# Strided attention on one core: VectorE's stream as a loop, two groups placed at once, ten single stores

## The chip, the cores and the metric

The kernel runs on one core of one Trainium2 chip. Its time is what the device takes for one launch, in microseconds (us). The core has five engines with instruction streams of their own: TensorE (PE; its weight loads are shown as PEld), VectorE (DVE), ScalarE (ACT), GpSimd (POOL) and SyncE (SP), which here issues all transfers. Sixteen DMA engines move the data between HBM and the on-chip memory (SBUF); matmul results lie in PSUM.

## The reference, cut to what matters

Every query attends to 16 keys alone, the rows 0, 64, 128, ... of its head:

```python
batch, heads, seq, dim = 8, 12, 1024, 64          # float32, stride 64
attend_positions = np.arange(0, seq, stride)      # 16 positions
...
scores  = np.einsum('bhqd,bhkd->bhqk', q, k) / np.sqrt(dim)
weights = np.exp(scores - np.max(scores, axis=-1, keepdims=True))
weights = weights / (np.sum(weights, axis=-1, keepdims=True) + 1e-10)
result[:, :, i, :] = np.einsum('bhqk,bhkd->bhqd', weights, v)[:, :, 0, :]
```

All of Q is read (25.2 MB), all of the result is written (25.2 MB), and only 0.8 MB of K and V is needed.

## The kernel before, in words

The 96 heads are worked on in 24 groups of four. A group's queries are 1 MB. They are loaded into one of 16 buffers (`big`), and the result of the group is later written over them and stored from there. So the loads of groups 0 to 15 can be issued at once, and the loads of groups 16 to 23 wait until the store that frees their buffer has landed.

One group g goes through the engines like this:

- ACT (`cast_a`) and POOL (`cast_p`) each cast half of the queries to bfloat16 (`qb`).
- VectorE transposes them (`turn_over`, `qt`, L353).
- TensorE forms the scores with the keys (`score_products`, L507). POOL copies the keys of the group from `k_all` to a small tile beforehand (`place_k`, L357).
- VectorE transposes the scores out of PSUM (`spread`, L373) and takes the maximum (L378). POOL subtracts it (L383), ACT takes the exponential (L389), VectorE adds up (L394) and takes the reciprocal (L399), POOL multiplies (`normalise`, L403), and VectorE transposes the weights back (`weights_back`, `w_t`, L409).
- TensorE forms the output products in two halves (L521) with the values that POOL has placed (`place_v`, L363). ACT copies each half from PSUM into the group's buffer (`evict`, L421), and SP stores it (L34).

The order of the work is written out by hand. A loop over steps n runs in the program that builds the kernel; step n does for VectorE: `spread(n)`, `turn_over(n+1)`, `maximum(n)`, `add_up(n-1)`, `weights_back(n-2)`, `invert(n-1)`. The other engines have their own lists in the same step. Each engine executes its list in order; waits between engines are worked out by `plan()`: an operation waits on a semaphore that counts the finished operations of another engine, or on a named one ("gate") that counts one kind of operation alone (`turned`, `wt`, `ev`, `stK`, `stV`).

TensorE's stream is the only one that loops on the chip: after two small products for the values and the scores of groups 0 to 2 comes a loop over groups 0 to 19, two per pass (`round_`, L529 and following). A round does the scores of group g+3 and then the two output halves of group g. Each pass ends with five subtractions from the gates (L552) and the loop's counter and branch (L548). Groups 20 to 23 follow as straight code, the last three without scores.

The stores are issued in the order of the list `order` (L444): groups 0 and 1 one by one, all others two at a time, with the loads of groups 16 to 23 in between. The store of groups 20 and 21 waits for an ACT operation that isn't a gate's; the first such one behind the evictions of group 21 is the first eviction of group 23. The store of groups 22 and 23 is issued last, and the program ends when it has landed.

`addr_align` (L145) places the start of the streams of ACT, VectorE and POOL at a multiple of 128 instructions.

Of the kernel before, what the change touches and what calls it, by code (L numbers as in the profile page):

```python
# [42 lines left out]
class Program:  # L43
# [13 lines left out]
    def op(self, engine, fn, reads=(), writes=(), after=(), lane=None, gate=None, gates=(), looped=False, last=False):  # L57
# [12 lines left out]
        for k in writes:  # L70
# [3 lines left out]
            gate=gate, gates=gates, last=last, looped=looped or engine == "PE",  # L74
# [3 lines left out]
    def plan(self):  # L78
# [43 lines left out]
        for i, o in enumerate(self.ops):  # L122
            transfer = o["lane"] != o["engine"]
            o["step"] = 16 if transfer else int(i in signals or o["engine"] == "PE" or o["last"])
# [7 lines left out]
        return counts, list(carriers)  # L132

    def emit(self, loops):
        nc = self.nc
        engines = {
# [6 lines left out]
        with self.tc.tile_critical(no_gpsimd_drain=True):  # L143
            for e in ("ACT", "DVE", "POOL"):
                engines[e].addr_align(128, max_nops=0)  # L145
            for o in self.ops:
                if o["looped"]:
                    continue
                for gate, n in o["gates"]:
                    engines[o["engine"]].wait_ge(gates[gate], n)  # L150
                for d in o["waits"]:
                    p = self.ops[d]
                    engines[o["engine"]].wait_ge(sems[p["lane"]], p["count"])
                r = o["fn"]()
                if o["gate"]:
                    r.then_inc(gates[o["gate"]], 1)
                elif o["step"]:
                    r.then_inc(sems[o["lane"]], o["step"])
# [8 lines left out]
def kernel(  # L167
# [14 lines left out]
    P = 128  # L182
# [6 lines left out]
    TURN = 2  # L189
    AHEAD = 3  # L190
    LOOPED = 20
# [20 lines left out]
    k_cur = [sb.tile([P, 2, 2, 32], BF16, name=f"k_cur{i}") for i in range(2)]  # L212
    v_cur = [sb.tile([P, 4, D], BF16, name=f"v_cur{i}") for i in range(2)]
# [25 lines left out]
    def store(g, n):  # L239
        b = g % NB  # L240
        op("SP", lambda: send(g, n), lane="out8" if n < 2 and b % 2 else f"out{b // 2}",
           reads=[f"b{i % NB}{h}" for i in range(g, g + n) for h in "ab"])
# [109 lines left out]
    def turn_over(g):  # L352
        op("DVE", lambda: nc.vector.transpose(qt[g % 2].bitcast(I32), qb[g % 4].bitcast(I32)),  # L353
           reads=[f"qb{g % 4}0", f"qb{g % 4}1"], writes=[f"qt{g % 2}"], gate="turned")

    def place_k(g):
        op("POOL", lambda: nc.gpsimd.tensor_copy(  # L357
            out=k_cur[g % 2].rearrange("p f b x -> p (f b x)").bitcast(I32),
            in_=k_all[:, g].rearrange("p f b x -> p (f b x)").bitcast(I32),
        ), reads=["k_zero"] + [f"k{g % 2}{s}" for s in range(4)], writes=[f"k_cur{g % 2}"], gate="stK")  # L360

    def place_v(g):
        op("POOL", lambda: nc.gpsimd.tensor_copy(  # L363
            out=v_cur[g % 2].rearrange("p x d -> p (x d)").bitcast(I32),
            in_=v_all[:, g].rearrange("p x d -> p (x d)").bitcast(I32),
        ), reads=[f"v_all{g % 2}{x}" for x in range(4)], writes=[f"v_cur{g % 2}"], gate="stV")

    def scores(g):
        op("PE", None, reads=[f"qt{g % 2}", f"k_cur{g % 2}"], writes=[f"sc{g % 2}"],
           gates=[("turned", g + 1), ("stK", g + 1)])  # L370

    def spread(g):
        op("DVE", lambda: nc.vector.transpose(  # L373
            s_t[g % 2].rearrange("p n k -> p (n k)"), sc_ps[g % 2],
        ), reads=[f"sc{g % 2}"], writes=[f"s_t{g % 2}"])

    def maximum(g):
        op("DVE", lambda: nc.vector.tensor_reduce(  # L378
            out=top[g % 2], in_=s_t[g % 2], op=ALU.max, axis=mybir.AxisListType.X,
        ), reads=[f"s_t{g % 2}"], writes=[f"top{g % 2}"])  # L380
# [7 lines left out]
    def raise_(g):  # L388
        op("ACT", lambda: nc.scalar.activation(  # L389
            out=ex[g % 2][:, :, 0:NK], in_=diff[g % 2], func=AF.Exp, bias=0.0, scale=scale,  # L390
        ), reads=[f"diff{g % 2}"], writes=[f"ex{g % 2}"])

    def add_up(g):
        op("DVE", lambda: nc.vector.tensor_reduce(  # L394
            out=total[g % 2], in_=ex[g % 2], op=ALU.add, axis=mybir.AxisListType.X,
        ), reads=[f"ex{g % 2}"], writes=[f"total{g % 2}"])

    def invert(g):
        op("DVE", lambda: nc.vector.reciprocal(rec[g % 2], total[g % 2]),  # L399
           reads=[f"total{g % 2}"], writes=[f"rec{g % 2}"])  # L400

    def normalise(g):
# [3 lines left out]
        ), reads=[f"ex{g % 2}", f"rec{g % 2}"], writes=[f"w_n{g % 2}"])  # L406

    def weights_back(g):
        op("DVE", lambda: nc.vector.transpose(  # L409
            _ap_with(w_t[g % 2], [w_t[g % 2].ap[0], [64, 8], [1, 2], [2, 32]]),  # L410
            w_n[g % 2].rearrange("p n k -> p (n k)"),
        ), reads=[f"w_n{g % 2}"], writes=[f"w_t{g % 2}"], gate="wt")

    def outputs(g, h):
        op("PE", None, reads=[f"w_t{g % 2}", f"v_cur{g % 2}"], writes=[f"o{h}"],
           gates=[("ev", 2 * g + h + 1)] + ([("wt", g + 1), ("stV", g + 2)] if h == 0 else []))
# [15 lines left out]
    for s in range(4):  # L432
# [11 lines left out]
    order = [("S", 0, 1), ("S", 1, 1), ("S", 2, 2), ("L", 16, 1), ("L", 17, 1), ("S", 4, 2), ("L", 18, 1), ("L", 19, 1),  # L444
             ("S", 6, 2), ("L", 20, 1), ("L", 21, 1), ("S", 8, 2), ("L", 22, 1), ("L", 23, 1)]
# [14 lines left out]
    def on(f, g, *a):  # L460
        if 0 <= g < NG:
            f(g, *a)

    for n in range(NG + 4):
        on(evict, n - 3, 1)
        if n < NG:
            spread(n)
        if n == 0:
            maximum(n)
        on(turn_over, n + 1)  # L470
        if n == 0:
            value_blocks(0, range(2, 4))
        elif n < NG:
            maximum(n)
        on(add_up, n - 1)
        on(weights_back, n - 2)
        on(invert, n - 1)
# [6 lines left out]
        on(scores, n + 1)  # L484
# [14 lines left out]
    def pe_stream(sems, gates):  # L499
        pe = nc.tensor  # L500

        def score_products(g):
            for f in range(2):
                for e in range(2):
                    for b in range(2):
                        c = 2 * b + e
                        r = pe.matmul(  # L507
                            sc_ps[g % 2][32 * c : 32 * c + 32], lhsT=k_cur[g % 2][:, f, b],
# [6 lines left out]
            r.then_inc(sems["PE"], 1)  # L515

        def output_products(g, h):
            for t in range(4):
                for b in range(2):
# [4 lines left out]
                        rhs=v_cur[g % 2][half_b].rearrange("p x d -> p (x d)"),  # L524
# [3 lines left out]

        def round_(g, less, more):  # L529
            if more:  # L530
                pe.wait_ge(gates["turned"], g + AHEAD + 1 - less)
                pe.wait_ge(gates["stK"], g + AHEAD + 1 - less)
                score_products(g + AHEAD)
            for h in range(2):
                pe.wait_ge(gates["ev"], 2 * (g - less) + h + 1)
                if h == 0:
                    pe.wait_ge(gates["wt"], g - less + 1)
                    pe.wait_ge(gates["stV"], g - less + 2)
                output_products(g, h)
# [4 lines left out]
        for g in range(AHEAD):  # L544
            pe.wait_ge(gates["turned"], g + 1)
            pe.wait_ge(gates["stK"], g + 1)
            score_products(g)
        with pe.Fori(0, LOOPED // TURN):  # L548
            for j in range(TURN):
                round_(j, 0, True)  # L550
# [46 lines left out]
```

## Time and profile before

| | us |
|---|---|
| median of 3 runs | 127.99 (127.95 to 128.06) |
| the profiled execution | 128.59 |
| its span, first to last instruction | 126.8 |
| busy: DVE / ACT / POOL / PE | 100.0 / 90.1 / 86.7 / 64.8 |
| moved by DMA | 51.18 MB, mean 404 GB/s over the span |

A page of the profile has these parts: the busy time of each engine, the span in 40 slices, the DMA queues, the chain of work that ended last (followed back from the last instruction), groups of instructions by line, and DMA issues by line. "DVE qt L353" is an operation of VectorE that writes the tile `qt`, issued by line 353. A table by stretches gives for each stretch the busy time of PE, PEld, DVE, ACT and POOL in us with the number of instructions, then TensorE's granted clock, the share of the 16 DMA engines that was busy, and GB/s. A row "x2: 558/592/627, 31.1 to 34.8" of one line's instructions means two of them, with minimum, median and maximum duration in ns, and the start of the first and the last in us; "DMA to landing" is the time from such an issue to its last byte's arrival. An engine's name with a q (DVEq, PEldq, SPq) means a step that its sequencer does alone.

### The profile page before, as it was taken

The numbers are of one execution on the slowest core, as the hardware profiler recorded it, in microseconds if no ns is written. First come the engines' busy times: TensorE is split into PE (matmuls) and PEld (weight loads), VectorE is DVE, ScalarE is ACT, GpSimd is POOL, SyncE is SP. The second block draws the span as 40 slices with busy tenths as digits, with TensorE's granted clock in tenths as the row PEclk, the third lists the DMA queues.
The fourth block names the chain that finished last, engine by engine and source line by source line (L and its number), as shares of the span: only waits on it lengthen the run. The fifth ranks groups of instructions, "written<-read, shape, count | busy, mean of one in ns | idle before, by whom it ended". The sixth has DMA issues, their size and how long they took to land.

```text
span 126.8 us, 1795 instructions
## 1 busy us (share of the span) xinstructions
PE 64.8 (51%) x580; PEld 33.7 (27%) x580; DVE 100.0 (79%) x159; ACT 90.1 (71%) x106; POOL 86.7 (68%) x132
## 2 busy tenths in 40 slices
PE   0000713277788777779535478877774537910000
PEld 0000100043344543334222234454331225500000
DVE  4329699999999999999999999999999997200000
ACT  4025778579988889988999988888997877840000
POOL 4016742899999999999999999999999685200000
PEclk9999999999999999999999655555559995596555
DMA  2999999999999999999998999999899999999991
GB/s 59 341 406 432 455 413 444 434 413 465 393 444 444 403 385 447 413 460 408 413 450 357 424 481 401 393 470 424 382 429 426 424 429 429 413 434 424 424 398 57
DMA packets 6230, 51.18 MB, mean 404 GB/s; under 512 B 3696, under 2 KB 3696, under 8 KB 3696
## 3 DMA queue, kind: packets, MB, share of 16 engines
q1 hardware_dynamic: 6224, 51.12, 96.7%
q14 instruction: 5, 0.04, 0.2%
q8 instruction: 1, 0.02, 0.0%
HBM read 25.95 MB, written 25.17 MB: 403 GB/s over the span
## 4 chain that ended last, share of the span: by engine, by line
DVE 70%; DMA 6%; ACT 5%; PE 3%; SPq 2%; issue 1%; POOL 1%
DVE qt L353 20%; DVE w_t L409 12%; DVE total L394 11%; DVE s_t L373 11%; DVE top L378 11%; DMA big<-in_V_dram 6%; DVE rec L399 4%; ACT big L421 3%; PE o L521 3%; DVE v_all L331 2%; SPq L34 1%; ACT qb L344 1%; PE o L307 1%; POOL big L315 1%; ACT big L323 1%
## 5 line engine op out<-in xcount | busy, mean ns | idle before, releaser
L521 PE MATMUL o<-v_cur,w_t 64*64 64x256 bf16 x384 | 40.9, 379 | 22.0 <-ACT big L421 13.3
L421 ACT COPY big<-o 128x1024 f32<-128x1024 f32 x48 | 46.3, 1015 | 7.4 <-PE o L521 7.1
L521 PEld LDWEIGHTS o<-v_cur,w_t 64*64 64x64 bf16 x384 | 30.0, 148 | 41.6 <-ACT big L421 30.0
L403 POOL TENSOR_TENSOR w_n<-ex,rec 128x512 bf16<-128x512 f32 x24 | 25.4, 1057 | 7.5 <-DVE rec L399 7.5
L507 PE MATMUL sc<-qt,k_cur 128*32 128x512 bf16 x192 | 23.2, 576 | 11.9 <-DVE qt L353 11.8
L383 POOL TENSOR_TENSOR diff<-s_t,top 128x512 f32<-128x512 f32 x24 | 25.4, 1060 | 5.6 <-DVE top L378 5.6
L353 DVE STREAM_TRANSPOSE qt<-qb 128x1024 int32<-128x1024 int32 x24 | 29.1, 1212 | 0.0
L349 POOL CAST qb<-big 128x1024 bf16<-128x1024 f32 x24 | 25.3, 1053 | 0.1
L344 ACT CAST qb<-big 128x1024 bf16<-128x1024 f32 x24 | 25.2, 1054 | 0.0
L409 DVE STREAM_TRANSPOSE w_t<-w_n 128x512 bf16<-128x512 bf16 x24 | 18.2, 759 | 1.3 <-POOL w_n L403 1.2
L389 ACT ACTIVATE ex<-diff 128x512 f32<-128x512 f32 x24 | 15.3, 639 | 5.2 <-POOL diff L383 5.2
L394 DVE TENSOR_REDUCE total<-ex 128x32 f32<-128x544 f32 x24 | 17.2, 718 | 0.3 <-ACT ex L389 0.3
L373 DVE STREAM_TRANSPOSE s_t<-sc 128x512 f32<-128x512 f32 x24 | 16.1, 670 | 0.0
L378 DVE TENSOR_REDUCE top<-s_t 128x32 f32<-128x512 f32 x24 | 15.8, 659 | 0.1
L507 PEld LDWEIGHTS sc<-qt,k_cur 128*32 128x32 bf16 x192 | 3.2, 104 | 22.6 <-DVE qt L353 22.6
L307 PE MATMUL o<-big,perm_v 128*128 128x384 bf16 x4 | 1.5, 521 | 12.7 <-POOL big L315 12.7
L399 DVE RECIPROCAL rec<-total 128x32 f32<-128x32 f32 x24 | 7.7, 320 | 0.0
L357 POOL COPY k_cur<-k_all 128x64 int32<-128x64 int32 x24 | 5.7, 237 | 2.1 <-ACT k_all L300 1.8
L363 POOL COPY v_cur<-v_all 128x128 int32<-128x128 int32 x24 | 7.1, 294 | 0.0
L290 ACT CAST big<-big 128x384 bf16<-128x384 f32 x1 | 0.5, 512 | 5.4 <-DMA big<-in_K_dram 5.4
L291 POOL CAST big<-big 128x384 bf16<-128x384 f32 x1 | 0.5, 509 | 5.1 <-DMA big<-in_K_dram 5.1
L307 PEld LDWEIGHTS o<-big,perm_v 128*128 128x128 bf16 x4 | 0.4, 131 | 13.1 <-POOL big L315 12.7
(18 smaller groups left out, 18.9 us busy)
## 6 DMA issues: line engine op xcount, KB each, us to landing
big<-in_Q_dram SPq DMA_DIRECT2D x24, 1024.0 KB, 14.0
out_dram<-big SPq DMA_DIRECT2D x11, 2048.0 KB, 16.3
out_dram<-big SPq DMA_DIRECT2D x2, 1024.0 KB, 16.6
big<-in_K_dram SPq DMA_DIRECT2D x1, 384.0 KB, 6.6
big<-in_V_dram SPq DMA_DIRECT2D x1, 384.0 KB, 8.0
```

Of the source, the lines that this page charges most:

```text
L344: op("ACT", lambda: nc.scalar.copy(b[:, half:], q[:, half:]), reads=[f"b{g % NB}{h}" for h in "ab"], writes=[f"qb{g % 4}1"])
L349: op("POOL", lambda: nc.gpsimd.tensor_copy(out=b[:, 0:half], in_=q[:, 0:half]), reads=[f"b{g % NB}{h}" for h in "ab"], writes=[f"qb{g % 4}0"])
L353: op("DVE", lambda: nc.vector.transpose(qt[g % 2].bitcast(I32), qb[g % 4].bitcast(I32)), reads=[f"qb{g % 4}0", f"qb{g % 4}1"], writes=[f"q ...
L373: op("DVE", lambda: nc.vector.transpose(s_t[g % 2].rearrange("p n k -> p (n k)"), sc_ps[g % 2],), reads=[f"sc{g % 2}"], writes=[f"s_t{g % ...
L378: op("DVE", lambda: nc.vector.tensor_reduce(out=top[g % 2], in_=s_t[g % 2], op=ALU.max, axis=mybir.AxisListType.X,), reads=[f"s_t{g % 2}"] ...
L383: op("POOL", lambda: nc.gpsimd.tensor_tensor(out=diff[g % 2], in0=s_t[g % 2], in1=top[g % 2].unsqueeze(2).to_broadcast([P, 32, NK]), op=AL ...
L394: op("DVE", lambda: nc.vector.tensor_reduce(out=total[g % 2], in_=ex[g % 2], op=ALU.add, axis=mybir.AxisListType.X,), reads=[f"ex{g % 2}"] ...
L403: op("POOL", lambda: nc.gpsimd.tensor_tensor(out=w_n[g % 2], in0=ex[g % 2][:, :, 0:NK], in1=rec[g % 2].unsqueeze(2).to_broadcast([P, 32, N ...
L409: op("DVE", lambda: nc.vector.transpose(_ap_with(w_t[g % 2], [w_t[g % 2].ap[0], [64, 8], [1, 2], [2, 32]]), w_n[g % 2].rearrange("p n k -> ...
L421: op("ACT", lambda: nc.scalar.copy(to, o), reads=[f"o{h}"], writes=[f"b{g % NB}{'ab'[h]}"], gate=None if g == NG - 1 else "ev")
L507: r = pe.matmul(sc_ps[g % 2][32 * c : 32 * c + 32], lhsT=k_cur[g % 2][:, f, b], rhs=_ap_with(qt[g % 2], [qt[g % 2].ap[0], [D, 8], [16 * D, ...
L521: r = pe.matmul(o_ps[h][half_b, t // 2, 256 * (t % 2) : 256 * (t % 2) + 256], lhsT=w_t[g % 2][half_b, 4 * h + t], rhs=v_cur[g % 2][half_b] ...
```

## The change

- VectorE's steps 2 to 21 are a loop on the chip: five passes of four rounds (`dve_stream`). The steps 0 and 1 stand ahead of it and the steps from 22 on behind it, as straight code. The loop waits on gates alone: new ones count score products (`sc`), POOL's casts (`qp`), exponentials (`ex`), normalised weights (`wn`) and VectorE's own transposes and sums (`own`). Each pass ends with five subtractions from them.
- So that `qp` stands for both halves of a cast, POOL's cast of group g waits for ACT's as well (from group 3 on).
- POOL places keys and values for two groups at once, every second group (from group 2 on), into four tiles instead of two; in its step `place_k` comes first and `place_v` ahead of `normalise`. TensorE no longer waits on `stK` and `stV` in its rounds.
- TensorE's loop covers all 24 groups, four per pass, with three subtractions. The rounds of groups 21 to 23 therefore do score products too, for groups that do not exist; they read the tiles as they are, and nothing reads what they write. VectorE releases them with three `nop`s behind its reciprocal of group 22.
- Groups 0 to 9 are stored one by one; each buffer's store has a semaphore of its own.
- POOL's stream starts 112 instructions behind a multiple of 128.

```diff
-            for e in ("ACT", "DVE", "POOL"):
-                engines[e].addr_align(128, max_nops=0)
+            for e, at in (("ACT", 0), ("DVE", 0), ("POOL", 112)):
+                engines[e].addr_align(128, offset=at, max_nops=0)
...
-    TURN = 2
+    TURN = 4
+    FIRST, LAST, ROUNDS = 2, 22, 4
     AHEAD = 3
-    LOOPED = 20
...
-           reads=[f"b{g % NB}{h}" for h in "ab"], writes=[f"qb{g % 4}0"])
+           reads=[f"b{g % NB}{h}" for h in "ab"] + [f"qb{g % 4}1"] * (g > FIRST), writes=[f"qb{g % 4}0"], gate="qp")
...
+    def place(to, from_, g, n, needs, writes):
+        dims = " ".join("pgabx"[: len(to.shape)])
+        flat = f"{dims} -> p ({dims[2:]})"
+        op("POOL", lambda: nc.gpsimd.tensor_copy(
+            out=to[:, g % 4 % 2 : g % 4 % 2 + n].rearrange(flat).bitcast(I32),
+            in_=from_[:, g : g + n].rearrange(flat).bitcast(I32),
+        ), reads=needs, writes=writes)
+
+    def pair(g):
+        return 1 if g < 2 else 0 if g % 2 else 2
...
-    order = [("S", 0, 1), ("S", 1, 1), ("S", 2, 2), ("L", 16, 1), ("L", 17, 1), ("S", 4, 2), ("L", 18, 1), ("L", 19, 1),
-             ("S", 6, 2), ("L", 20, 1), ("L", 21, 1), ("S", 8, 2), ("L", 22, 1), ("L", 23, 1)]
+    order = [("S", 0, 1), ("S", 1, 1)]
+    for g in range(2, 10, 2):
+        order += [("S", g, 1), ("S", g + 1, 1), ("L", NB + g - 2, 1), ("L", NB + g - 1, 1)]
     order += [("S", g, 2) for g in range(10, 22, 2)]
...
+        if n == NG - 1:
+            for g in range(AHEAD):
+                op("DVE", lambda: nc.vector.nop(), gate="turned", late=True)
+        on(place_k, n + 2)
         on(cast_p, n + 2)
         if n < NG:
             subtract(n)
+        on(place_v, n - 1)
         on(normalise, n - 1)
-        on(place_k, n + 2)
-        on(place_v, n - 1)
...
-        with pe.Fori(0, LOOPED // TURN):
+        with pe.Fori(0, NG // TURN):
             for j in range(TURN):
-                round_(j, 0, True)
-            for name, n in (("turned", 1), ("stK", 1), ("stV", 1), ("wt", 1), ("ev", 2)):
+                pe.wait_ge(gates["turned"], j + AHEAD + 1)
+                score_products(j + AHEAD)
+                for h in range(2):
+                    pe.wait_ge(gates["ev"], 2 * j + h + 1)
+                    if h == 0:
+                        pe.wait_ge(gates["wt"], j + 1)
+                    output_products(j, h)
+            for name, n in (("turned", 1), ("wt", 1), ("ev", 2)):
                 pe.sem_inc(gates[name], -n * TURN)
-        for g in range(LOOPED, NG):
-            round_(g, LOOPED, g + AHEAD < NG)
...
+    def dve_stream(sems, gates):
+        dve = nc.vector
+        with dve.Fori(0, (LAST - FIRST) // ROUNDS):
+            for j in range(ROUNDS):
+                g = FIRST + j
+                dve.wait_ge(gates["sc"], g + 1)
+                lay(g).then_inc(gates["own"], 1)
+                dve.wait_ge(gates["qp"], g + 2)
+                turn(g + 1).then_inc(gates["turned"], 1)
+                dve.wait_ge(gates["own"], 2 * j + 1)
+                highest(g).then_inc(sems["DVE"], 1)
+                dve.wait_ge(gates["ex"], g)
+                sums(g - 1).then_inc(gates["own"], 1)
+                dve.wait_ge(gates["wn"], g - 1)
+                back(g - 2).then_inc(gates["wt"], 1)
+                dve.wait_ge(gates["own"], 2 * j + 2)
+                inverse(g - 1).then_inc(sems["DVE"], 1)
+            for name in ("sc", "qp", "ex", "wn"):
+                dve.sem_inc(gates[name], -ROUNDS)
+            dve.sem_inc(gates["own"], -2 * ROUNDS)
+        prog.rest(sems, gates, {name: LAST - FIRST for name in ("sc", "qp", "ex", "wn")})
```

`lay`, `turn`, `highest`, `sums`, `back` and `inverse` issue the same instructions as `spread`, `turn_over`, `maximum`, `add_up`, `weights_back` and `invert` before.

More of the change, by code (lines that the diff above doesn't have):

```diff
@@ L143, in emit @@
         with self.tc.tile_critical(no_gpsimd_drain=True):
-            for e in ("ACT", "DVE", "POOL"):
-                engines[e].addr_align(128, max_nops=0)
+            for e, at in (("ACT", 0), ("DVE", 0), ("POOL", 112)):
+                engines[e].addr_align(128, offset=at, max_nops=0)
             for o in self.ops:
[L147 to L158, printed above, removed]
+                if not o["looped"] and not o["late"]:
+                    self.put(o, sems, gates, {})
             nc.sync.wait_ge(sems["ACT"], counts["ACT"])
@@ L362, in place_v @@
-    def place_v(g):
[L363 to L366, printed above, removed]
-    def scores(g):
[L369 to L375, printed above, removed]
@@ new lines, in place_v, with lay @@
+    def place_v(g):
+        n = pair(g)
+        if n:
+            place(v_two[g % 4 // 2], v_all, g, n,
+                  [f"v_all{i % 2}{x}" for i in range(g, g + n) for x in range(4)],
+                  [f"v_cur{i % 4}" for i in range(g, g + n)])
+    def scores(g):
+        op("PE", None, reads=[f"qt{g % 2}", f"k_cur{g % 4}"], writes=[f"sc{g % 2}"],
+           gates=[("turned", g + 1)], gate="sc")
+    def lay(g):
+        return nc.vector.transpose(s_t[g % 2].rearrange("p n k -> p (n k)"), sc_ps[g % 2])
```

135 lines of the change are left out of this document (78 added, 57 removed).

## The prediction

> **What bounds the kernel now.** I read the page from the top: span, DMA queues, the chain that ended last. Then the stretches at the end, where engines have stopped.
>
> ```profile
> span 126.8 us, 1795 instructions
> q1 hardware_dynamic: 6224, 51.12, 96.7%
> DVE 70%; DMA 6%; ACT 5%; PE 3%; SPq 2%; issue 1%; POOL 1%
> ```
>
> The chain says VectorE (DVE), 70% of the span. The queue line says that data packets alone fill 96.7% of 16 engines' span. Both cannot set the end, so I look at what runs last.
>
> ```profile
> 104.00:108.00 4.00, 2.65 (x24) 1.95 (x24) 2.88 (x6) 3.32 (x4) 2.73 (x4) 0.59 1.01 422
> 112.00:116.00 4.00, 0.00 (x0) 0.00 (x0) 0.00 (x0) 0.46 (x1) 0.00 (x0) 0.87 1.02 434
> 123.00:123.50 0.50, 0.00 (x0) 0.00 (x0) 0.00 (x0) 0.00 (x0) 0.00 (x0) 0.50 0.77 328
> 123.50:124.00 0.50, 0.00 (x0) 0.00 (x0) 0.00 (x0) 0.00 (x0) 0.00 (x0) 0.50 0.47 197
> 124.00:124.50 0.50, 0.00 (x0) 0.00 (x0) 0.00 (x0) 0.00 (x0) 0.00 (x0) 0.50 0.23 98
> 124.50:125.00 0.50, 0.00 (x0) 0.00 (x0) 0.00 (x0) 0.00 (x0) 0.00 (x0) 0.50 0.23 98
> ```
>
> The columns are PE, PEld, DVE, ACT and POOL busy, granted clock, DMA share, GB/s. From 112.5 us nothing computes; the ring of stores drains at full share until 123. Then DMA engines drop out one after another: the shares after 123 add to 0.85 us per engine ((0.77+0.47+0.23+0.23) x 0.5), while the last lands at 126.0. Fewer than four of 16 engines carry the last microsecond. So the bound is the DMA ring, and at its end its slowest engines. The compute chain enters only through the moment at which the last stores are issued:
>
> ```profile
> L34 SPq DMA_DIRECT2D out_dram<-big x1: 538/538/538, 102.8 to 102.8; - x1
> DMA to landing us min/median/max: 13.5/13.5/13.5
> L34 SPq DMA_DIRECT2D out_dram<-big x1: 539/539/539, 111.6 to 111.6; - x1
> DMA to landing us min/median/max: 9.5/9.5/9.5
> L34 SPq DMA_DIRECT2D out_dram<-big x1: 539/539/539, 112.8 to 112.8; - x1
> DMA to landing us min/median/max: 13.2/13.2/13.2
> ```
>
> These are the stores of groups 18 and 19, 20 and 21, 22 and 23. They land at 116.3, 121.1 and 126.0, 4.9 us apart, which is 2 MB at ring speed. How late may the second be issued? An empty ring needs a while from issue to first packet:
>
> ```profile
> 0.96 0.39 SPq L258 DMA_DIRECT2D big<-in_Q_dram  x1
> 0.96:1.95 0.99, 0.00 (x0) 0.00 (x0) 0.07 (x1) 0.63 (x1) 0.30 (x2) 1.00 0.00 0
> 1.95:2.10 0.15, 0.00 (x0) 0.00 (x0) 0.15 (x1) 0.15 (x1) 0.15 (x1) 1.00 3.10 382
> ```
>
> Issued at 0.96, first packets after 1.95: 1.0 us. With 4.9 us of transfer and about 0.4 us to the landing, issue plus 6.3 us. To land by 121.1 it must be issued by 114.8. It is issued at 111.6: **the compute chain has 3.2 us to spare**, no more.
>
> **The change, part by part.** *Time base.* The profiled execution took 128.59 us, 1.8 outside its 126.8 span; the median is 127.99, 0.6 lower. I sum against the landing at 126.0 and carry the difference to 127.99.
>
> *VectorE's loop.* Rounds 2 to 21 keep their six instructions; five passes add each five semaphore subtractions, a counter step and a branch. VectorE has no idle time in a round:
>
> ```profile
> 40.67 0.72 DVE L394 TENSOR_REDUCE total<-ex 128x32 f32<-128x544 f32 x1
> 41.29 0.76 DVE L409 STREAM_TRANSPOSE w_t<-w_n 128x512 bf16<-128x512 bf16 x1
> 41.94 0.32 DVE L399 RECIPROCAL rec<-total 128x32 f32<-128x32 f32 x1
> 42.16 0.66 DVE L373 STREAM_TRANSPOSE s_t<-sc 128x512 f32<-128x512 f32 x1
> ```
>
> The reciprocal waits for the sum, which ends as w_t starts (41.29). Only then can the sequencer pass it and reach the subtractions. What follows is covered until s_t is due at 42.16: 0.87 us. No row shows this on VectorE; the nearest are TensorE's loop and VectorE's own two sequencer steps at the end:
>
> ```profile
> L552 PEldq EVENT_SEMAPHORE  x5: 51/51/51, 98.6 to 99.2; - x5
> L548 PEldq COMPARE_BRANCH  x1: 76/76/76, 99.5 to 99.5; - x1
> L532 PEldq EVENT_SEMAPHORE  x1: 51/51/51, 100.0 to 100.0; - x1
> L592 DVEq EVENT_SEMAPHORE  x1: 21/21/21, 126.3 to 126.3; - x1
> L592 DVEq DRAIN  x1: 10/10/10, 126.4 to 126.4; - x1
> ```
>
> A subtraction takes 0.15 us on TensorE (0.6 over four steps) and about 0.1 on VectorE, five of them 0.5 to 0.75. Counter and branch: 0.2 if each is such a step, up to 0.6 by TensorE (99.4 to 100.0). Together 0.7 to 1.35, so 0 to 0.5 us shows per pass. A harder bound is VectorE's first branch at 1.0, after which its first instruction starts at 1.88: 0.9 for the branch alone, 1.4 to 1.65 in all, up to 0.8 exposed. I take 0.2 x 5 = **1.0 us** (bounds 0 and 4), nearer to VectorE's own row. All of it moves every later group, because round follows round without a gap.
>
> *TensorE's loop over all groups.* Groups 21 to 23 now have a score product ahead of their output products, on old data, released by three no-operations that VectorE issues behind the reciprocal of group 22. Queued behind it are the outputs, then ACT's evictions, then the store of 20 and 21.
>
> ```profile
> 92.90 1.05 PE L507 MATMUL sc<-qt,k_cur 128*32 128x512 bf16 x8
> 100.41 0.65 PE L507 MATMUL sc<-qt,k_cur 128*32 128x512 bf16 x8 [0.80 <-DVE qt L353]
> 103.63 0.71 DVE L394 TENSOR_REDUCE total<-ex 128x32 f32<-128x544 f32 x1
> 105.10 1.91 PE L521 MATMUL o<-v_cur,w_t 64*64 64x256 bf16 x16 [1.73 <-DVE w_t L409]
> 107.26 1.98 PE L521 MATMUL o<-v_cur,w_t 64*64 64x256 bf16 x16 [0.25 <-ACT big L421]
> 109.43 1.98 PE L521 MATMUL o<-v_cur,w_t 64*64 64x256 bf16 x16 [0.19 <-ACT big L421]
> ```
>
> The no-operations can go when the sum of group 22 is done (103.63+0.71); with 0.1 for the step and 0.4 from TensorE's wait to its matmuls (100.0 to 100.41) the first extra product starts near 104.85. At the half clock of this stretch (0.59 in the row of 104 to 108) it takes 1.05 us, to 105.9: 0.8 behind the present 105.10. The next two groups stand 2.16 us apart now, set by ACT's evictions; TensorE would need 1.91+1.05 = 2.96, so 0.8 more each. Upper bound 2.4. At full clock 1.06+0.65 (outputs and scores there) fits into 2.16, lower bound 0. Since one product's end overlaps the next one's start I take **1.9 us**. The subtractions that TensorE saves (three per four groups instead of ten) lie where it waits for data anyway.
>
> *Sum of the chain.* 1.0+1.9 = 2.9 us, against 3.2 to spare: it just fits.
>
> *POOL.* Two groups' keys and values now go in one copy:
>
> ```profile
> L403 POOL TENSOR_TENSOR w_n<-ex,rec 128x512 bf16<-128x512 f32 x24 | 25.4, 1057 | 7.5 <-DVE rec L399 7.5
> L363 POOL COPY v_cur<-v_all 128x128 int32<-128x128 int32 x24 | 7.1, 294 | 0.0
> ```
>
> Half of the copies go and the rest grow, which saves under 0.29 us per group. Against it stands a second wait in the cast, one sequencer step, for an ACT cast issued a round earlier, hence done. POOL idles 0.31 us a group (7.5/24) until VectorE's reciprocal, so both are worth nothing: VectorE's full round hides them. If that cover went, one step of 0.1 against the saving would still cost nothing.
>
> *Instruction loads.* These compete on the ring:
>
> ```profile
> q14 instruction: 1, 0.01, 1.0%
> q14 instruction: 1, 0.01, 1.9%
> q8 instruction: 1, 0.02, 3.1%
> ```
>
> They fall at 78 to 80, 95 to 96 and 105 to 107 us; by share x 16 x window 0.3, 0.3 and 1.0 us of one DMA engine. Which engine each is for, no row says; I assign the first two to VectorE and POOL, whose straight code is the longest, and the third, of another size, to TensorE, which is then in the tail behind its loop. Counted in the code, VectorE's stream shrinks from some 170 instructions to some 85: its load goes. POOL starts near a block's end and loads early instead. TensorE's straight code (57 instructions, then four rounds of 48) reaches the length it had at 105 us on its first pass, near 39 us: that load moves, it doesn't go. As several engines end together, taking one load from one of them need not move the end. Ring value **0**; bounds -1.7 (all 16 engines end together, at 123+0.85) and +1.4 (a load lands on the slowest engine).
>
> *Single stores.*
>
> ```profile
> L34 SPq DMA_DIRECT2D out_dram<-big x2: 558/592/627, 31.1 to 34.8; - x2
> DMA to landing us min/median/max: 16.0/16.6/17.3
> ```
>
> Groups 0 and 1 are single already: landings at 48.4 and 50.8, 2.4 us per MB, like half of 4.9. Eight more cost **0.1** at most, and 4 x 0.56 us of SP, which idles. The Trainium skill ("DMA: Bandwidth & Descriptors", Bandwidth) gives a fixed 2.0 us per DMA; by it four more would cost 8 us. The landings 2.4 us apart disagree: with the ring full the fixed part is hidden.
>
> **Forecast and rivals.** *No change, 128.0 us*: ring 0 to +0.1, chain 0.3 short of its spare. Chance 0.35.
>
> *Slower: VectorE's back branch.* From an exposed 0.26 us per pass (1.3 in all) the store of 20 and 21 sets the end; at 0.4 it is 2.0+1.9-3.2 = +0.7, **128.7 us**, at 0.8 +2.7. For it: VectorE is full in every row, so nothing absorbs the loss; the 0.9 us behind its first branch. Against it: the sequencer overlaps with two instructions. Chance 0.32.
>
> *Faster: the ring's ends draw together.* If two of the late loads go and the clock leaves the extra products cheap, the slow engines end 0.6 earlier, **127.4 us**. The chain then must hold: with 0.3 for the loop it allows issue at 113.8 and a last landing at 113.8+6.3+4.9 = 125.0. For it: the shares after 123. Against: early loads delay an engine just as late ones do, since the ring is never empty. Chance 0.29.
>
> *TensorE reloads its code on each back branch.* Its loop may straddle two blocks. Five passes of a 1.0 us load on one DMA engine: +5 less what that engine has in hand (up to 1.7), **132 us**. Against it: the present loop shows no load per pass. The Trainium skill ("Runtime: NRT & Kernel Launch", Instruction fetch mechanics) says that a taken branch to a page outside the two held forces such a load; no run here shows it. Chance 0.04.
>
> **The numbers.** About 0.2% (0.26 us) is what a measurement of this kernel can tell from no change. Faster 0.29, same 0.35, slower 0.36. The likeliest case alone holds 127.7 to 128.3; the range takes in most of the faster and of the slower case: 127.2 to 129.5.
>
> **What would show it.** The store of 20 and 21 should be issued at 113.5 to 115, and land at 121 to 122. A gap between reciprocal and s_t every fourth round shows the price of a pass: 0 to 0.5. An instruction load near 39 us and none at 79. Outputs of group 21 near 107. I am wrong if the ring's engines end within 1 us of each other, or if the gap is above 0.3.

## The result, and the profile after

The changed kernel took 128.79 us (median of 11 runs, 128.20 to 129.52) beside 128.06 us of the kernel before (11 runs, 127.91 to 128.53): a ratio of 1.0063, 95% interval 1.0048 to 1.0079. It is **slower by 0.6%**. The time lies inside the predicted range, but "no change", the likeliest single case (0.35), did not come, and what made it slower is none of the causes that the prediction gave for "slower". That the range held it is luck.

First the page of the changed kernel: span, data queue, the chain that ended last (shares of the span by engine), the instruction queues, and the stores by size (count, KB each, median us to landing).

```profile
span 127.2 us, 1802 instructions
q1 hardware_dynamic: 6800, 51.12, 96.3%
q14 instruction: 3, 0.02, 0.1%
q8 instruction: 1, 0.02, 0.0%
DVE 67%; DMA 6%; ACT 4%; PE 4%; issue 3%; SPq 2%; POOL 1%; DVEq 0%
out_dram<-big SPq DMA_DIRECT2D x7, 2048.0 KB, 16.4
out_dram<-big SPq DMA_DIRECT2D x10, 1024.0 KB, 17.3
```

The same bytes go in 6800 packets instead of 6224, because eight groups more are stored one by one: 512 packets more of data, and 16 small ones for each of the four transfers more. Four instruction loads are left of six. The chain looks much as before, and as before it does not set the end. The profiled execution took 129.25 us, 2.05 outside its span; before it was 128.59 and 1.8.

The same stretches as in the prediction (PE, PEld, DVE, ACT and POOL busy, granted clock, DMA share, GB/s):

```profile
104.00:108.00 4.00, 3.28 (x32) 1.69 (x32) 3.11 (x6) 3.23 (x5) 2.80 (x4) 0.64 0.99 422
112.00:116.00 4.00, 0.00 (x0) 0.00 (x0) 0.00 (x0) 0.79 (x1) 0.00 (x0) 0.92 0.99 418
123.00:123.50 0.50, 0.00 (x0) 0.00 (x0) 0.00 (x0) 0.00 (x0) 0.00 (x0) 0.50 0.47 197
123.50:124.00 0.50, 0.00 (x0) 0.00 (x0) 0.00 (x0) 0.00 (x0) 0.00 (x0) 0.50 0.31 131
124.00:124.50 0.50, 0.00 (x0) 0.00 (x0) 0.00 (x0) 0.00 (x0) 0.00 (x0) 0.50 0.16 66
124.50:125.00 0.50, 0.00 (x0) 0.00 (x0) 0.00 (x0) 0.00 (x0) 0.00 (x0) 0.50 0.08 33
125.00:125.50 0.50, 0.00 (x0) 0.00 (x0) 0.00 (x0) 0.00 (x0) 0.00 (x0) 0.50 0.08 33
```

A row counts a packet in the stretch where it begins. The shares after 123 add to 0.55 us per engine; before it was 0.85. The ring as a whole finishes *earlier* in this execution, and still the last engine ends later: the row of 125.0 to 125.5 has 0.08, one packet begun on one engine, where before it has 0.00. In this execution the average did not grow, the slowest engine did.

The stores of groups 20 and 21, and 22 and 23 (start of the issue; then the time to landing):

```profile
L34 SPq DMA_DIRECT2D out_dram<-big x1: 539/539/539, 111.9 to 111.9; - x1
DMA to landing us min/median/max: 9.6/9.6/9.6
L34 SPq DMA_DIRECT2D out_dram<-big x1: 539/539/539, 113.2 to 113.2; - x1
DMA to landing us min/median/max: 13.3/13.3/13.3
```

Issued at 111.9, only 0.3 later than before and far from the limit of 114.8. The last landing is at 113.2 + 13.3 = 126.4 (126.0 before). So the compute chain, in which the prediction put 2.9 us, kept nearly all of its spare time.

### The profile page after: what moved, and what is told of

The parts are those of the page before. It is cut to its first block, busy times and chain, and to the rows that moved or that the text cites. A ratio compares the mean times of both kernels' runs of the same rounds, so it can differ in the third digit from the quotient of the medians.

```text
span 127.2 us, 1802 instructions
## 1 busy us (share of the span) xinstructions
PE 62.2 (49%) x604; PEld 31.8 (25%) x604; DVE 100.4 (79%) x159; ACT 90.2 (71%) x106; POOL 84.4 (66%) x110
## 4 chain that ended last, share of the span: by engine, by line
DVE 67%; DMA 6%; ACT 4%; PE 4%; issue 3%; SPq 2%; POOL 1%; DVEq 0%
DVE qt L363 20%; DVE s_t L399 12%; DVE total L424 11%; DVE top L406 11%; DVE w_t L444 9%; DMA big<-in_V_dram 6%; DVE rec L431 3%; ACT big L460 3%; PE o L566 2%; DVE v_all L341 2%; SPq L34 1%; PE sc L552 1%; ACT qb L354 1%; PE o L317 1%; POOL big L325 1%
## 5 line engine op out<-in xcount | busy, mean ns | idle before, releaser
L566 PE MATMUL o<-v_two,w_t 64*64 64x256 bf16 x384 | 36.9, 350 | 21.7 <-DVE w_t L444 21.3
L566 PEld LDWEIGHTS o<-v_two,w_t 64*64 64x64 bf16 x384 | 27.8, 138 | 40.4 <-ACT big L460 23.6
L552 PE MATMUL sc<-qt,k_two 128*32 128x512 bf16 x216 | 24.8, 548 | 15.1 <-DVE qt L363 14.0
L552 PEld LDWEIGHTS sc<-qt,k_two 128*32 128x32 bf16 x216 | 3.6, 102 | 26.2 <-DVE qt L363 24.3
L372 POOL COPY k_two<-k_all 128x128 int32<-128x128 int32 (+1 forms) x13 | 3.7, 282 | 2.1 <-ACT k_all L310 1.8
L372 POOL COPY v_two<-v_all 128x256 int32<-128x256 int32 (+1 forms) x13 | 4.9, 380 | 0.0
L303 DVE STREAM_TRANSPOSE big<-big 128x384 int32<-128x384 int32 x1 | 0.6, 578 | 4.0 <-POOL big L301 4.0
```

Of the source, the lines that this page charges most:

```text
L552: r = pe.matmul(sc_ps[g % 2][32 * c : 32 * c + 32], lhsT=k_cur[g % 4][:, f, b], rhs=_ap_with(qt[g % 2], [qt[g % 2].ap[0], [D, 8], [16 * D, ...
L566: r = pe.matmul(o_ps[h][half_b, t // 2, 256 * (t % 2) : 256 * (t % 2) + 256], lhsT=w_t[g % 2][half_b, 4 * h + t], rhs=v_cur[g % 4][half_b] ...
```

## The experiments

Three theories stood at the start. *Theory 1*: TensorE's instruction load, moved from 105.8 to 42.5 us, puts one DMA engine behind for good. *Theory 2*: VectorE's branches and the extra scores. *Theory 3*: the stores of groups 2 to 9 one by one. The profile after speaks for theory 1, since the 16 engines' landings of one transfer lie 1.0 us apart until that load and 2.3 behind it. All kernels compute the whole reference; the extra scores of experiment 4 are never read.

**1. The load alone, in the kernel before.** TensorE's instructions are shifted.

```
+            engines["PE"].addr_align(256, offset=120, max_nops=0)
             for e in ("ACT", "DVE", "POOL"):
```

> The kernel before, with TensorE's instructions alone shifted by an alignment ahead of them (120 slots past a block of 256), so that its 16 KB instruction load should come in the first pass of its loop, near 40 us, instead of at 105.8. Nothing else changes. Theory 1 (the early load puts one DMA engine of the ring behind, and it stays behind to the end): the spread of the 16 engines at a store's landing rises from 1.1 to about 2 at the load, and the end comes 0.3 to 0.8 us later, ratio 1.003 to 1.006. Theory 2 (branches of VectorE's loop and the extra scores) and theory 3 (the stores one by one): neither is in this kernel, so ratio 1.000.

Measured: 1.0008 (0.9984 to 1.0031). The load came at 34.1 us, and the landings of one store spread from 0.9 to 2.2 us just as theory 1 says; the time of the twelve runs did not follow. The expected 1.003 to 1.006 did not come, though the interval reaches 1.0031. Only one of the twelve was profiled (128.80 us).

**2. The load out of the way, in the changed kernel.** The same line with an offset of 249.

> The changed kernel, with TensorE's instructions alone shifted so that a block of 256 slots begins some 7 instructions behind its first one and holds the whole loop: the load should come in the first 2 us, or there is none before 110. Theory 1: the spread stays near 1.1 to 57 us, the end returns to that of before or earlier, ratio 0.994 to 1.001. Theories 2 and 3: as the changed kernel, ratio 1.006.

Measured: 1.0081 (1.0047 to 1.0114), with the load at 5.6 us instead of in the first 2. Not faster. (Two of its ten runs had 2.9 and 3.4 us outside the span, the others 1.9 to 2.4; this I cannot explain.) Theory 1 does not get its gain here either.

**3. Pairs again, in the changed kernel.**

```
-    order = [("S", 0, 1), ("S", 1, 1)]
-    for g in range(2, 10, 2):
-        order += [("S", g, 1), ("S", g + 1, 1), ("L", NB + g - 2, 1), ("L", NB + g - 1, 1)]
+    order = [("S", 0, 1), ("S", 1, 1), ("S", 2, 2), ("L", 16, 1), ("L", 17, 1), ("S", 4, 2), ...
```

> The changed kernel with the stores of groups 2 to 9 in pairs again, in the order of before. Theory 3 (the single stores make packets uneven over the engines at 55 to 58 us, where the spread of the changed kernel rose from 2.3 to 2.9): ratio 1.000 to 1.003. Theory 1: the load near 42 us remains, ratio 1.004 to 1.007. Theory 2: 1.006.

Measured: **1.0000** (0.9977 to 1.0022). VectorE's loop, TensorE's loop, POOL's pairs and the early load (at 38.7 us) are all in it, and it costs nothing that these runs can tell against before. Its page:

```profile
out_dram<-big SPq DMA_DIRECT2D x11, 2048.0 KB, 16.1
out_dram<-big SPq DMA_DIRECT2D x2, 1024.0 KB, 17.6
```

**4. The extra scores alone, in the kernel before.**

```
-    LOOPED = 20
+    LOOPED = NG
+        if n == NG - 1:
+            for g in range(AHEAD):
+                for name in ("turned", "stK"):
+                    op("DVE", lambda: nc.vector.nop(), gate=name)
```

> The kernel before with TensorE's loop over all 24 groups (three extra scores on old data, released by no-operations of VectorE), still two groups to a pass: its code is then so short that no load should come in the run. Theory 2 (the extra scores stand in the chain): the store of groups 20 and 21 is issued 1 to 2 us later than 111.6, ratio 1.000 to 1.006. Theory 1: the store is issued within 0.4 us of before, and without the load at 105.8 the slowest engine ends up to 0.8 us earlier, ratio 0.994 to 1.000.

Measured: 0.9991 (0.9974 to 1.0008). No TensorE load is left in the run. TensorE's timeline at the end (start, length, what), and the issue of the store of 20 and 21:

```profile
104.36 0.85 PE L512 MATMUL sc<-qt,k_cur 128*32 128x512 bf16 x8 [1.28 <-DVEq L487]
105.14 1.91 PE L526 MATMUL o<-v_cur,w_t 64*64 64x256 bf16 x16
106.98 1.05 PE L512 MATMUL sc<-qt,k_cur 128*32 128x512 bf16 x8
107.96 1.08 PE L526 MATMUL o<-v_cur,w_t 64*64 64x256 bf16 x16
```

```profile
L34 SPq DMA_DIRECT2D out_dram<-big x1: 538/538/538, 111.5 to 111.5; - x1
```

The first extra score fills a gap in which TensorE waited anyway (1.73 us in the row of 105.10 of before), and the outputs start at 105.14. The second does push the outputs of group 22 to 107.96 (107.26 before), but they then take 1.08 us instead of 1.98, and the store goes out at 111.5, as before.

**5. The changed kernel once more,** beside the next three on one chip.

> The changed kernel itself, once more, beside the three others on one chip. All theories: 1.004 to 1.008 as before; at 1.002 or less the difference would belong to the chip or to the day and not to the kernel.

Measured: 1.0077 (1.0052 to 1.0103). In this execution TensorE's load came at 111.6 us instead of 42.5, from the same program:

```profile
q8 instruction: 1, 0.02, 3.1%
```

(the window of 111 to 113 us). So the place of that load is not settled by the kernel's text alone. This execution took 128.48 us, the quickest of the six; where the load fell in the other five is not known. So the run shows that the difference belongs to the kernel, and does not decide theory 1.

**6. Single stores alone, in the kernel before:** the order of experiment 3 reversed, and `lane=f"out{b}"`.

> The kernel before with the stores of groups 2 to 9 one by one, in the order and on the semaphores of the changed kernel, and nothing else of the change. Theory 3 (single stores): 8 groups of 8 KB packets at 311 ns in place of 16 KB packets at 616 cost each DMA engine 6 ns per 16 KB, 0.2 us in all, and four more landings; with uneven packets in the stretch of mixed loads and stores up to 0.8, so ratio 1.003 to 1.006. Theory 1 and theory 2: 1.000.

Measured: **1.0059** (1.0030 to 1.0087). This one edit gives nearly the whole difference, with TensorE's load at 106.1 us, late as before, in its profile. So theory 1 is not the cause of it: the loss is there without the early load (here), and in experiment 3 the load is early and the loss is not there. A smaller share of the load is not excluded. Worked out from the landing records, the seven profiles with the load at 34 to 43 us end 0.41 us later than the seven others (0.39 either way at 95%), one execution each; four of the first seven have single stores, and three of the others. The page's stores, and the end of the ring:

```profile
out_dram<-big SPq DMA_DIRECT2D x7, 2048.0 KB, 17.2
out_dram<-big SPq DMA_DIRECT2D x10, 1024.0 KB, 16.5
```

```profile
124.00:124.50 0.50, 0.00 (x0) 0.00 (x0) 0.00 (x0) 0.00 (x0) 0.00 (x0) 0.50 0.31 131
124.50:125.00 0.50, 0.00 (x0) 0.00 (x0) 0.00 (x0) 0.00 (x0) 0.00 (x0) 0.50 0.31 131
125.00:125.50 0.50, 0.00 (x0) 0.00 (x0) 0.00 (x0) 0.00 (x0) 0.00 (x0) 0.50 0.16 66
```

More packets begin after 124.5 than in the kernel before, which is down to 0.23 and then 0.00. The edit also moves other transfers: a store goes out as soon as its own group is done, and the loads behind it with it. Here the loads of groups 18 and 19, first in this run, then before:

```profile
53.09 3.44 SPq L34 DMA_DIRECT2D big<-in_Q_dram  x2
```

```profile
56.05 1.11 SPq L34 DMA_DIRECT2D big<-in_Q_dram  x2
```

**7. The changed kernel without VectorE's loop.** The looped instructions are written out in the same order, on the same gates.

```
-        how = dict(looped=FIRST <= n < LAST, late=n >= LAST)
+        how = {}
-    pending, sems = prog.emit([dve_stream, pe_stream])
+    pending, sems = prog.emit([pe_stream])
```

> The changed kernel with VectorE's stream written out instead of a loop, everything else as changed. Theory 2 (VectorE's branches): the store of groups 20 and 21 is issued 0.3 to 0.5 us earlier than 111.9, and if this counts the ratio falls from 1.006 to 1.002 to 1.004. Theory 3: stays 1.004 to 1.008. Theory 1: VectorE's instruction load near 79 us is back and hits one more DMA engine, 1.004 to 1.009.

Measured: 1.0066 (1.0045 to 1.0086). VectorE's loop is not the cause. Its price is read where the branch lies, between reciprocal and s_t. First the changed kernel at the ends of two passes, then this one at the second of these places:

```profile
38.05 0.30 DVE L431 RECIPROCAL rec<-total 128x32 f32<-128x32 f32 x1
38.32 0.72 DVE L399 STREAM_TRANSPOSE s_t<-sc 128x512 f32<-128x512 f32 x1
...
53.20 0.31 DVE L431 RECIPROCAL rec<-total 128x32 f32<-128x32 f32 x1
53.45 0.72 DVE L399 STREAM_TRANSPOSE s_t<-sc 128x512 f32<-128x512 f32 x1
```

```profile
53.20 0.31 DVE L431 RECIPROCAL rec<-total 128x32 f32<-128x32 f32 x1
53.43 0.66 DVE L399 STREAM_TRANSPOSE s_t<-sc 128x512 f32<-128x512 f32 x1
```

From start to start 0.27 and 0.25 with the branch, 0.23 without, and s_t itself is 0.06 longer: at most 0.1 us a pass, 0.5 in all, in a chain that has 3 to spare. The store of 20 and 21 was issued at 111.3 here, 0.6 before 111.9, but in experiment 5 it was issued at 111.3 with the loop.

**8. TensorE's load at the entry of its loop:** the line of experiment 2 with an offset of 202.

> The changed kernel with TensorE's instructions shifted so that the block of 256 slots begins at the loop's entry: its 16 KB load should come at 25 to 32 us, where the ring carries loads alone, instead of 42.5. Theory 1 in its narrower form (it is the engine's lag in the stretch of mixed loads and stores that counts): no change from the changed kernel, 1.004 to 1.008. Theory 3: the same. A load that is nearly free there, as POOL's of 0.3 us at 14: spread 1.3 at 40 us and ratio 1.002 to 1.005.

Measured: 1.0058 (1.0039 to 1.0076), the load at 35.2 us and not at 25 to 32. As the changed kernel.

**9. Single stores behind the mixed stretch.** Groups 2 to 9 as in experiment 3, and

```
-    order += [("S", g, 2) for g in range(10, 22, 2)]
+    order += [("S", g, 1) for g in range(10, 22)]
```

> The changed kernel with groups 2 to 9 stored in pairs (as before) and groups 10 to 21 one by one instead: twelve single stores in place of eight, all but the first behind the stretch in which loads and stores mix. If it is the single stores in the mixed stretch that count: spans as before (126.6 to 126.8 in the mean). If each single store costs the ring, wherever it stands: twelve against eight, spans 0.6 to 0.9 longer than before. It has 45 semaphores against 43 of the changed kernel and 35 of before: if their number sets the time outside the span (1.78 before, 1.97 changed), that is 1.97 or more here.

Measured: 1.0066 (1.0041 to 1.0092), from six runs. Of the 0.82 us between the means, 0.34 lies outside the span (2.12 against 1.78), 0.48 inside. Neither expectation on the span holds: it is not "as before", and twelve stores do not cost more than eight. Its profiled execution happens to be a quick one (span 126.7) and shows the ring at its usual rate: the stores of groups 10 to 19 land from 93.9 to 116.1 us, 2.46 us apart, half of the 4.92 that pairs take. So where its other runs lose time is not shown.

**10. The single stores on fewer semaphores.**

```
-        op("SP", lambda: send(g, n), lane=f"out{b}",
+        op("SP", lambda: send(g, n), lane=f"out{b % 8}",
```

> The changed kernel with its single stores on eight semaphores in turn instead of thirteen (the store of group 8 takes that of group 0, which has landed long before): 38 semaphores in all. If the number of semaphores sets the time outside the span: 1.78 to 1.80 instead of 1.97, ratio 1.004 to 1.006; else 1.9 to 2.0 as in the changed kernel. Spans as in the changed kernel, 0.5 longer than before.

Measured: 1.0049 (1.0032 to 1.0065). Outside the span 1.79, as said; span 0.59 longer than before, as said.

**11. Fewer alternations of loads and stores, in the kernel before.**

```
-    order = [..., ("S", 2, 2), ("L", 16, 1), ("L", 17, 1), ("S", 4, 2), ("L", 18, 1), ("L", 19, 1),
-             ("S", 6, 2), ("L", 20, 1), ("L", 21, 1), ("S", 8, 2), ("L", 22, 1), ("L", 23, 1)]
+    order = [..., ("S", 2, 2), ("L", 16, 1), ("L", 17, 1), ("L", 18, 1), ("L", 19, 1),
+             ("S", 4, 2), ("S", 6, 2), ("S", 8, 2), ("L", 20, 1), ("L", 21, 1), ("L", 22, 1), ("L", 23, 1)]
```

> The kernel before with the same pairs and loads in fewer alternations: the four loads of groups 16 to 19 behind the stores of 2 and 3, then the stores of 4 to 9, then the four loads of 20 to 23. If slow load packets come from each change between stores and loads, there are half as many: 0.2 to 0.4 us less extra time at 44 to 92 us, ratio 0.994 to 0.999. If they come with every load that other engines' stores run beside: 0.999 to 1.002. If the later loads come late: 1.003 or more.

Measured: 0.9986 (0.9970 to 1.0003), which does not decide between the first two expectations. In its profile the engines end closest together, with nothing left after 124.5 (first and last row with a share):

```profile
123.00:123.50 0.50, 0.00 (x0) 0.00 (x0) 0.00 (x0) 0.00 (x0) 0.00 (x0) 0.50 0.62 262
...
124.00:124.50 0.50, 0.00 (x0) 0.00 (x0) 0.00 (x0) 0.00 (x0) 0.00 (x0) 0.50 0.16 66
```

**12. Experiments 4 and 11 together,** as a candidate that might beat both kernels.

> The kernel before with two edits together: TensorE's loop over all 24 groups (its code then needs no instruction load in the run) and the loads of groups 16 to 23 in two blocks of four, as the two kernels that ran at 0.9991 and 0.9986. If what each takes off the slowest engine of the ring adds: 0.997 to 0.998, with the engines of the last landing within 1.0 to 1.5 us of each other. If the slowest engine is a matter of chance whatever the order: 0.999 to 1.000, and a spread of 1.6 to 2.4.

Measured: 1.0008 (0.9998 to 1.0017). It doesn't: the two hints of a gain, neither of them clear of 1, do not add up, the engines of the last landing are 2.5 us apart, and no version here is shown to be faster than before.

All runs in one table. "Semaphores" are those that the kernel itself allocates. "Span" is the mean over the runs less that of the kernel before in the same comparison; "outside" is device time less span, in the mean (1.78 for the kernel before in each comparison):

```
                            semaphores   ratio    span us   outside us
pairs in groups 2 to 9
  1  load at 34                     35   1.0008     +0.11      1.79
  3  changed, pairs                 40   1.0000     -0.04      1.79
  4  extra scores                   35   0.9991     -0.18      1.80
 11  two blocks of loads            35   0.9986     -0.15      1.78
 12  both                           35   1.0008     +0.09      1.79
  9  changed, singles 10 to 21      45   1.0066     +0.48      2.12
singles in groups 2 to 9
  5  changed                        43   1.0077     +0.64      1.96
  2  changed, load at 5.6           43   1.0081     +0.46      2.25
  8  changed, load at 35            43   1.0058     +0.58      1.89
  7  changed, no VectorE loop       42   1.0066     +0.71      1.91
 10  changed, fewer semaphores      38   1.0049     +0.59      1.79
  6  before, singles                39   1.0059     +0.73      1.79
```

Two causes stand out. **Single stores lengthen the span by 0.5 to 0.7 us. More semaphores lengthen the time outside it**: experiment 10 changes nothing but the semaphores of the stores, from 43 to 38 in all, and the time falls from 1.97 to 1.79. That it begins beyond 40, and an estimate of 0.04 to 0.07 us for each one more, are read from the rows (without experiment 2's 2.25); these kernels differ in other things too.

## Where the prediction was right and wrong

**The bound** was right. The end is set by the ring's slowest engines; the edits of the compute chain that experiments 3, 4 and 7 leave in or take out don't move it.

**VectorE's loop, 1.0 us**: too much. The rows of 53.20 and 53.45 give 0.02 to 0.1 a pass. These are the sequencer's steps there:

```profile
L610 DVEq EVENT_SEMAPHORE  x4: 21/21/21, 52.7 to 53.0; - x4
L611 DVEq EVENT_SEMAPHORE  x1: 21/21/21, 53.1 to 53.1; - x1
L594 DVEq ALU_OP  x1: 40/40/40, 53.2 to 53.2; - x1
L594 DVEq COMPARE_BRANCH  x1: 63/63/63, 53.2 to 53.2; - x1
```

The five subtractions run under w_t (52.55 to 53.30), as the lower bound had it, and the branch is over before s_t is due. The branch of 76 ns on TensorE that the prediction showed is the last of its loop, which is not taken; taken ones last 207 to 228 ns there.

**The extra scores, 1.9 us**: too much. I let the first extra score start at 104.85 and the outputs behind it; these are the rows:

```profile
104.66 0.67 PE L552 MATMUL sc<-qt,k_two 128*32 128x512 bf16 x8 [1.04 <-DVEq L521]
105.38 1.91 PE L566 MATMUL o<-v_two,w_t 64*64 64x256 bf16 x16
107.23 1.05 PE L552 MATMUL sc<-qt,k_two 128*32 128x512 bf16 x8
108.20 1.22 PE L566 MATMUL o<-v_two,w_t 64*64 64x256 bf16 x16
109.35 0.63 PE L552 MATMUL sc<-qt,k_two 128*32 128x512 bf16 x8
110.09 0.62 PE L566 MATMUL o<-v_two,w_t 64*64 64x256 bf16 x8
```

It takes 0.67, not 1.05, and the outputs start at 105.38 (105.10 before) instead of 105.9 to 107. From 108 on, 16 matmuls of the outputs take 1.22 us and 8 take 0.62, where 16 took 1.98 before. The granted clock differs there (the number before the last two), first before, then after:

```profile
108.00:111.00 3.00, 2.81 (x28) 1.63 (x24) 0.74 (x1) 2.52 (x4) 0.70 (x2) 0.50 0.99 421
```

```profile
108.00:111.00 3.00, 2.61 (x36) 1.38 (x32) 0.75 (x1) 2.38 (x4) 0.70 (x1) 0.91 0.99 421
```

The 1.9 took the half clock for nearly all of the three rounds. In the ten profiles with extra scores the clock of this stretch is 0.91 to 1.00, and the store of 20 and 21 is issued at 111.3 to 112.1; in the four without it is 0.50 to 0.53, and 111.5 to 111.6. Why the clock is higher with them is not shown, and what they cost at half clock to the end was not seen. The whole sum of 2.9 came to 0.3.

**POOL, nothing**: right.

```profile
L438 POOL TENSOR_TENSOR w_n<-ex,rec 128x512 bf16<-128x512 f32 x24 | 25.4, 1057 | 6.5 <-DVE rec L431 5.4
L372 POOL COPY v_two<-v_all 128x256 int32<-128x256 int32 (+1 forms) x13 | 4.9, 380 | 0.0
```

The copies fell from 7.1 to 4.9 us, and POOL still waits for VectorE's reciprocal.

**Instruction loads, 0**: not contradicted (what experiment 6 says of the early load leaves room for a share), and the loads moved nearly as said: VectorE's at 79 is gone (experiment 7, without its loop, has one again at 80.1), POOL's is early (14 us), TensorE's came at 42.5. Rows of 13 to 15 us and 42 to 44 us:

```profile
q14 instruction: 1, 0.01, 1.0%
```

```profile
q8 instruction: 1, 0.02, 3.2%
```

That it can come at 111.6 in another execution of the same program I hadn't thought of; why, no run shows. The rival of reloads at each back branch is out, as the page has one load on q8 in the whole run, for six branches of TensorE (the last not taken):

```profile
L580 PEldq COMPARE_BRANCH  x6: 76/210/228, 39.1 to 111.6; - x6
```

The first branch lies at 39.1, so the load at 42.5 falls in the loop's second pass, not in the first as predicted. The Trainium skill ("Runtime: NRT & Kernel Launch", Instruction fetch mechanics) says that a taken branch whose target lies outside the two pages held forces such a load. The trace has no load beside any of the five taken branches; what the one at 42.5 came for, it does not show.

**Single stores, 0.1 at most: this is the step that failed.** I priced them by the ring's rate, 2.4 us per MB, and the rate was right: packets of 8 KB follow each other in 307 ns, packets of 16 KB in 613, and experiment 9 shows singles 2.46 us apart. (The Trainium skill's fixed cost of about 2.0 us per transfer, in "DMA: Bandwidth & Descriptors", Anatomy of one DMA — SWDGE (gpsimd) path, which describes transfers issued from GpSimd, is not seen here, where SP issues them: single stores land 2.46 us apart, half of the 4.92 of pairs.) But I had just shown that the end hangs on the slowest engine and then gave this term a cost for the average one. Worked out from the landing records of the 14 profiles, one for each kernel of the table, one of before and one of the first run after:

```
last transfer's landing, mean over the profiles    pairs in 2 to 9 (7)   singles (7)
earliest of the 16 engines, us                             123.51           123.52
latest of the 16 engines, us                               125.87           126.31
growth of latest less earliest, from the store of
group 1 (near 51 us) to that of 10 and 11 (near 96)          0.75             1.27
```

In the mean the earliest engine is untouched and the latest 0.44 us later (0.38 either way at 95%). The growth differs by 0.53 (0.44 either way): engines drift apart more in the stretch where loads and stores alternate. Experiment 2's profile does not fit: its engines end only 1.9 us apart, and all of them late (124.25 to 126.15). That single stores cause the loss is shown by experiments 3 and 6, from both sides. **How** they do it stays open. The drift in the mixed stretch is a lead, not a proof: experiment 9 has pairs there and lost 0.48 all the same, and its one profile does not show where. Fewer alternations gave no gain that is clear of noise (experiments 11 and 12). A single store differs from half a pair in three things: packets of half the size, a transfer of its own, and the moment of its issue, which moves loads too. No run separates them; that the loads go out 3 us earlier is not needed for a loss, as experiment 9 leaves those in place.

**Outside the span**: not in the prediction at all. I carried the 1.8 us of before over unchanged. The changed kernel has 43 semaphores where before had 35, and pays 0.19 of its 0.7 us there (1.97 in the mean of its first 11 runs); experiment 10 has 38 and gives it back.

**The marks.** I named four: the store of 20 and 21 at 113.5 to 115 (it was 111.9: wrong), 0 to 0.5 us behind the reciprocal (0.02 to 0.1: right, at the low end), the load near 39 and none at 79 (42.5 and none: nearly right here; 111.6 in experiment 5), the outputs of group 21 near 107 (105.38: wrong). The store of 20 and 21 landed at 121.5, within the 121 to 122 named. What was to prove me wrong, engines ending within 1 us, did not come: they ended 3.1 apart.

**The rival "slower by the back branch", 128.7**, had the right number by the wrong road: it needed the store of 20 and 21 to go out after 114.8, and it went at 111.9. The faster rival failed: with no TensorE load at all, experiments 4 and 12 stand at 0.9991 and 1.0008, and the engines of their last landing are 2.5 us apart, against 2.3 before.

## What to carry to other kernels

When a profile shows that the slowest of many parallel queues sets the end, price every edit by what it does to the slowest queue, and test transfer size and order first: the streams of three compute engines were rewritten here at no cost that the runs can tell, and splitting the stores cost most of the 0.7 us. A trace that offers a clear culprit (a load, then a lag that stays) is still one execution; moving that load alone, in both kernels, took two runs and showed that the loss does not follow it. And compare device time with the span before explaining the span.

## What was not expected of the hardware

- The time outside the span was 1.78 to 1.80 us with 35 to 40 semaphores of the kernel's own, 1.91 with 42, 1.89 to 1.97 with 43 (2.25 in experiment 2) and 2.12 with 45. No trace here shows where it lies.
- The same program had TensorE's 16 KB instruction load at 42.5 us in one execution and at 111.6 in another, 1.0 us on one DMA engine each time. In experiments 4 and 12, whose loop covers all groups two at a time, there is none.
- In the profile of experiment 1 the load at 34 us parts the landings of one transfer from 0.9 to 2.2 us, and they do not close up again (2.8 at the end); the ratio of its runs is 1.0008 (0.9984 to 1.0031).
- TensorE's granted clock from 108 to 111 us is 0.91 to 1.00 in the ten profiles with extra scores and 0.50 to 0.53 in the four without.
- Five semaphore subtractions, a counter and a branch on VectorE cost at most 0.1 us a pass: the subtractions (52.7 to 53.1) run while a transpose of 0.75 us does.
